# A macaron feed-forward layer: residual updates of four groups moved to ScalarE and accumulating DMAs, one more group in seven products

## The chip, the cores and the metric

The kernel runs on one core of a Trainium2 chip. The metric is device time in microseconds of one execution. The kernel before takes 1795.06 us, the median of three executions (1794.87 to 1795.85). About 0.2% of that, 3.6 us, is what a measurement can tell from no change.

A core has a matrix engine (TensorE, PE in the profile; its weight loads are listed as PEld), a vector engine (VectorE, DVE), an engine for pointwise functions (ScalarE, ACT), a general engine (GpSimd, POOL) and an engine that here only issues DMAs (SyncE, SP). Each runs its own instructions in order and waits for the others by semaphores. TensorE writes only to PSUM, which has eight banks of 128 x 512 float32; the DMAs cannot reach PSUM.

## The reference

One decoder layer on a sequence of 1024 tokens, width 1024, hidden width 2816, all in float32. Cut to what matters:

```
h = modulate(rms_norm(x, ffn1_norm), sh1, sc1)
x = x + 0.5 * g1 * ((silu(h @ w_gate) * (h @ w_up)) @ w_down)      # first feed-forward
h = modulate(rms_norm(x, mix_norm), sh2, sc2)
b, c, v, u = split(h @ w_in)                                       # mixer: a gated convolution and
x = x + g2 * (concat(norm(conv(b, c, v)), norm(ssm(u))) @ w_out)   # a diagonal state-space model
h = modulate(rms_norm(x, ffn2_norm), sh3, sc3)
x = x + 0.5 * g3 * ((silu(h @ w_gate2) * (h @ w_up2)) @ w_down2)   # second feed-forward
y = rms_norm(x, final_norm)
# sh, sc, g: nine vectors of length 1024 from silu(cond) @ w_mod + b_mod
```

## The kernel before, in words

Activations lie transposed: the residual x is 8 tiles of 128 channels (d) by two halves of 512 tokens (h), in SBUF throughout. A float32 product is made of three matmuls on rounded parts: every weight and activation is split into a high half (ScalarE casts it) and a low half (VectorE subtracts the high half), and `mm3` issues high x high, high x low and low x high. So weights cost ScalarE and VectorE one instruction each per tile of 128 x 1024, the class `Weights` does that and hands the tiles out in order.

The hidden width is worked off in 11 groups of 256. A plain group g of the first feed-forward is `gate_up` (names fa{g}g and fa{g}u, 64 calls of `mm3`) and `down_both`, which calls `down` (fa{g}d, 32 calls). `down` makes four outputs of 128 x 512 at a time in four PSUM banks of a ring of six (`ps`), and when they are done, VectorE adds each, times a gate, to x. In this kernel that is one instruction per output, 16 per group.

From group SEVEN_FROM on (6 in the first feed-forward, 1 in the second) gate and up use `seven`: a two-by-two block product from seven block products instead of eight. It needs sums of weights, which GpSimd makes in `combine`, and sums of activations (S1 to S4), which `combos` makes on VectorE, ScalarE and GpSimd while the last plain group runs. Its down-projection (`down2`) follows within the next group.

Beside the first feed-forward there is side work, nearly all on VectorE, written as generators: `side1` prepares constants of the state-space model (`ssm_base`), then eight batches of tables (`ssm_batch`), each with matmuls named kp and tp on TensorE that read the tiles cl and bl of VectorE, and small stores to DRAM; in between it reduces six of the nine modulation vectors from 1 MB weight blocks (`mod_block`, tiles wm). `Clock` sets where side work stands in the program: every call of `mm3` ticks it, and every `period` ticks one step of the first generator is issued. The period is 4 in the down-projection of group 0, then 3 in gate and up and 8 in down. Before the last plain group all that is left of the side work is issued at once, its memory (`es1`) is released, and the combinations start. The framework that builds the program then orders each engine's instructions itself, so neighbours in the code need not be neighbours on an engine. All DMAs of this kernel are issued from SP's queue.

Of the kernel before, what the change touches and what calls it, by code (L numbers as in the profile page):

```python
# [13 lines left out]
F32 = mybir.dt.float32  # L14
F32R = mybir.dt.float32r
I32 = mybir.dt.int32
AF = mybir.ActivationFunctionType
ALU = mybir.AluOpType
# [3 lines left out]
P = 128  # L22
D = 1024
S = 1024
HALF = 512
# [6 lines left out]
CH = 16  # L32
TAU = 8

SEVEN_FROM = (6, 1)
J = S // TAU
NB = 8
GB = G // NB
# [16 lines left out]
class Clock:  # L55
# [7 lines left out]
    def after(self, ticks, fn):  # L63
        self.n += 1
        bisect.insort(self.due, (self.now + ticks, self.n, fn))
# [151 lines left out]
def hymba_layer(ctx: ExitStack, tc, x_d, wm1_d, wmod_d, gu1_d, gs1_d, wd1_d, win_d, wout_d, glu_d, gu2_d, gs2_d, wd2_d, cols_d, cond_d, lam_d, bc_d, out_d):  # L217
    nc = tc.nc
    V, A, T, SP = (InOrder(tc, e) for e in (nc.vector, nc.scalar, nc.tensor, nc.sync))
# [16 lines left out]
    pools = {}  # L236
# [11 lines left out]
    def ps(name):  # L248
        return mm_ps.tile([P, HALF], F32, tag="mm", name=name)
# [14 lines left out]
    gate = const.tile([P, 3, KT], F32, name="gate")  # L264
# [3 lines left out]
    def plain(arrays):  # L268
        for a in arrays:
            granules.extend([[(len(srcs), 2 * q), (len(srcs), 2 * q + 1)] for q in range(2)])  # L270
            srcs.append(a)

    def stream(gu, gs, wd, m):

        plain(a for g in range(m) for a in (gu[2 * g], gu[2 * g + 1], wd[g]))
        for g in range(m, NGRP):
            j = len(srcs)
            inner = m < g < NGRP - 1
            srcs.extend([gs[g - m, 0], wd[g - 1], gs[g - m, 1]] if inner else [gs[g - m, 0], gs[g - m, 1]])
            seven = [(i, c) for i in (j, j + 1 + inner) for c in Weights.SEVEN]  # L280
            seven = [seven[i : i + 2] for i in range(0, 14, 2)]
            if inner:
                granules.extend(seven[:1] + [[(j + 1, 2 * q), (j + 1, 2 * q + 1)] for q in range(2)] + seven[1:])
            else:
                granules.extend(seven)
        j = len(srcs)
        srcs.extend([wd[NGRP - 2], wd[NGRP - 1]])
        granules.extend([(i, 2 * q), (i, 2 * q + 1)] for q in range(2) for i in (j, j + 1))

    stream(gu1_d, gs1_d, wd1_d, SEVEN_FROM[0])  # L290
    plain([win_d[i] for i in range(8)] + [glu_d] + [wout_d[i] for i in range(4)])
    stream(gu2_d, gs2_d, wd2_d, SEVEN_FROM[1])
    ws = Weights((V, A, SP, nc.gpsimd), srcs, granules, 2)
# [3 lines left out]
    x = [[xt[k // 2][h][:, k % 2, :] for h in range(2)] for k in range(KT)]  # L297
    clock = Clock(4)
# [6 lines left out]
    def mm3(out, w, k, act, first, last, tok=slice(0, HALF), more=False):  # L305

        hi, lo = wsel(w, k)
        ah, al = (a[:, tok] for a in act)
        T.matmul(out, lhsT=hi, rhs=ah, start=first, stop=False, skip_group_check=more)
        T.matmul(out, lhsT=hi, rhs=al, start=False, stop=False, skip_group_check=more)  # L310
        T.matmul(out, lhsT=lo, rhs=ah, start=False, stop=last, skip_group_check=more)
        clock.tick()
# [146 lines left out]
    def down(h, wd, groups, n, name, after):  # L459

        for d0 in range(0, KT, 4):
            outs = [ps(f"{name}d{d}_{h}") for d in range(d0, d0 + 4)]
            for q, a_tiles in enumerate(groups):
                for fi in range(2):
                    for i, o in enumerate(outs):
                        mm3(o[:], wd[2 * q + d0 // 4], 4 * fi + i, a_tiles[fi, h], q == fi == 0, q == len(groups) - 1 and fi == 1)
            for i, o in enumerate(outs):
                d = d0 + i
                V.scalar_tensor_tensor(out=x[d][h], in0=o[:], scalar=gate[:, n, d : d + 1], in1=x[d][h], op0=ALU.mult, op1=ALU.add)
                if after is not None:  # L470
                    after(d, h)

# [9 lines left out]
    def combos(act, name, homes):  # L482

        blocks.clear()
        while act[1] is None or len(act[1]) < KT:
            yield
        (a11, a12), (a21, a22) = [(act[h][:4], act[h][4:]) for h in range(2)]
        blocks.update(A11=a11, A12=a12, A22=a22, S1=[], S2=[], S3=[], S4=[])
        G_ = nc.gpsimd
        for k in range(4):  # L490
            f22, f21, f11 = whole(a22[k], f"f22_{k}", V), whole(a21[k], f"f21_{k}", V), whole(a11[k], f"f11_{k}", V)
            V.tensor_tensor(out=f22[:], in0=f21[:], in1=f22[:], op=ALU.add)
            blocks["S1"].append(split_act(f22[:], f"{name}S1_{k}", homes[0]))
            yield
            V.tensor_tensor(out=f21[:], in0=f11[:], in1=f21[:], op=ALU.subtract)
            V.tensor_tensor(out=f11[:], in0=f22[:], in1=f11[:], op=ALU.subtract)
            blocks["S2"].append(split_act(f11[:], f"{name}S2_{k}", homes[1]))
            yield
            blocks["S3"].append(split_act(f21[:], f"{name}S3_{k}", homes[2]))
            yield  # L500
        while "free" not in blocks:
            yield
        for k in range(4):
            f12, s2 = whole(a12[k], f"f12_{k}"), whole(blocks["S2"][k], f"s2_{k}")
            G_.tensor_tensor(out=f12[:], in0=f12[:], in1=s2[:], op=ALU.subtract)
            blocks["S4"].append(split_act(f12[:], f"{name}S4_{k}", homes[3]))
            yield
# [75 lines left out]
    def sums_opened():  # L583
        es = ExitStack()
        ws.sums_pool = es.enter_context(tc.tile_pool(name="sums", bufs=1))
        pools["first"] = es.enter_context(tc.tile_pool(name="first", bufs=1))
        ws.pump()
        return es
# [6 lines left out]
    es1 = ExitStack()  # L595
# [147 lines left out]
    ws.open(ring1, 1)  # L743
    raw2 = es1.enter_context(tc.tile_pool(name="raw2", bufs=1))
    sb = es1.enter_context(tc.tile_pool(name="sb", bufs=1))
    ssm = {}
    bps = []

# [262 lines left out]
    def gate_up(act, name, a_tiles):  # L1011

        for fi in range(2):
            (wg,) = ws.take()
            pg = [proj(wg, act[h], f"{name}g{fi}_{h}") for h in range(2)]
            ws.free()
            (wu,) = ws.take()
            for h in range(2):
                pu = proj(wu, act[h], f"{name}u{fi}_{h}")
                gu_evac(fi, h, pg[h], pu, a_tiles, f"{name}_{fi}_{h}")  # L1020
            ws.free()

    def down_both(a_tiles, name):
        wd = ws.take(2)
        for h in range(2):
            down(h, wd, [a_tiles], 0, name, None)
        ws.free(2)

    down_both(a_tiles, "fa0")
    first_seven = SEVEN_FROM[0]  # L1030
    for g in range(1, first_seven):
        a_tiles = {}
        if g == first_seven - 1:
            while clock.side:
                clock.step()
            clock.period = 4
            es1.close()
            movs["B"] = es1.enter_context(tc.tile_pool(name="movB1", bufs=12))
            clock.side.append(combos(act1, "h1", "BBBA"))
            ws.retire(ring1)  # L1040
        else:
            clock.period = 3
        gate_up(act1, f"fa{g}", a_tiles)
        if g < first_seven - 1:
            clock.period = 8
        else:
            blocks["free"] = True
            ring1_open.close()
            sums_open = sums_opened()
        down_both(a_tiles, f"fa{g}")  # L1050
# [9 lines left out]
    for h in range(2):  # L1060
        down(h, [w[0], w[2], w[1], w[3]], [a_last, a_prev], 0, "fa10", after1)
# [306 lines left out]
    for dh in range(2):  # L1368
        wd = ws.take(2)
        for h in range(2):  # L1370
            for tok in PIECES[h] if dh else WHOLE:
                for i in range(4):
                    d = 4 * dh + i
                    o = ps(f"fb10d{d}_{h}_{tok.start}")
# [23 lines left out]
def _arrays(i):  # L1398
# [5 lines left out]
    for n in (1, 2):  # L1404
        g, u = _tiles(i[f"ffn{n}_w_gate"][0]), _tiles(i[f"ffn{n}_w_up"][0])
        a[f"wd{n}"] = i[f"ffn{n}_w_down"][0].reshape(NGRP, 2, P, 2, 512).transpose(0, 2, 3, 1, 4).reshape(NGRP, P, 2, 1024)
        m = SEVEN_FROM[n - 1]
        a[f"gu{n}"] = np.stack([g, u], axis=2).reshape(NF, P, 2, 1024)[: 2 * m]
# [40 lines left out]
```

## Time and profile before

| | |
|---|---|
| median of three executions | 1795.06 us |
| profiled execution | 1797.88 us |
| its span | 1796.1 us |
| busy in the span | PE 1728.8, DVE 1209.6, ACT 490.4, POOL 248.4 us |
| stretch of the change | 84.8 us (start of fa0d) to 458.97 us (start of fa6g) |

The profile is one execution. Its page gives busy times by engine, the span in 40 slices, and the chain of work that ended last. Lists in order of time have the start and the time taken in microseconds, the engine, the source line, the operation, output and inputs by the program's names without their numbers, the shape and the count; in square brackets stands how long the engine was idle before, and what ended that. Almost every line number is 101, the helper through which the engines are called, so the names tell the places. Groups of instructions have the total busy time, the mean of one in nanoseconds, and the idle time ahead of them. A window's row has busy times of the engines in it, the granted TensorE clock (1.00 is full speed), and the share of the 16 DMA engines.

### The profile page before, as it was taken

What the parts mean: (1) busy time and instruction counts of PE and PEld (TensorE: products, weight loads), DVE (VectorE), ACT (ScalarE), POOL (GpSimd) and SP (SyncE); (2) the same over time, 40 slices, a digit from 0 to 9 for tenths busy, and PEclk for the clock granted to TensorE, in tenths of its full rate; (3) what the DMA queues carried; (4) which work ended last, traced back from release to release, by engine and by line L of the source; (5) the groups of instructions that cost most, each with busy time, mean ns of one, the idle gap of its engine ahead of it and who ended that gap; (6) DMA issues with size and microseconds to landing.
All of it is one profiled execution on the core that took longest, in us unless ns stands there. A gap on an engine that the chain in (4) does not pass through costs nothing.

```text
span 1796.1 us, 20089 instructions
## 1 busy us (share of the span) xinstructions
PE 1728.8 (96%) x7772; PEld 1424.8 (79%) x7772; DVE 1209.6 (67%) x2170; ACT 490.4 (27%) x750; POOL 248.4 (14%) x155
## 2 busy tenths in 40 slices
PE   4998999999999999999999999799999999999996
PEld 3787887887888888888888887588888888888885
DVE  7999999977566556644657548855665566556546
ACT  4311212222322323332114324232232223222331
POOL 0000000005212121200000110621112111211211
PEclk9999999999999999999999999899999999999997
DMA  7624666510111213125752101011111111111102
GB/s 310 232 63 149 209 215 217 182 69 24 47 47 48 71 47 107 52 74 169 228 150 67 47 24 41 30 47 49 67 49 48 50 68 48 47 51 68 48 24 94
DMA packets 58738, 165.03 MB, mean 92 GB/s; under 512 B 14353, under 2 KB 29969, under 8 KB 43922
## 3 DMA queue, kind: packets, MB, share of 16 engines
q1 hardware_dynamic: 58642, 163.74, 26.6%
q8 instruction: 61, 1.00, 0.2%
q14 instruction: 35, 0.29, 0.1%
HBM read 140.64 MB, written 18.87 MB: 89 GB/s over the span
## 4 chain that ended last, share of the span: by engine, by line
PE 83%; DVE 11%; POOL 2%; DMA 2%; ACT 1%; issue 1%; SPq 1%; DVEq 0%; ACTq 0%; POOLq 0%
PE wo L101 5%; PE b L101 2%; PE v L101 2%; PE u L101 2%; PE c L101 2%; PE fb10d L101 2%; PE fa10d L101 2%; DVE w L101 2%; PE fa2d L101 1%; PE fa4u L101 1%; PE fa2u L101 1%; PE fa5u L101 1%; PE fa0d L101 1%; PE fb8d L101 1%; PE fb7d L101 1%; PE fb6d L101 1%
## 5 line engine op out<-in xcount | busy, mean ns | idle before, releaser
L101 ACT CAST w<-raw 128x1024 fp32r<-128x1024 f32 (+1 forms) x203 | 171.6, 860 | 489.2 <-POOL raw L159 61.3
L101 DVE TENSOR_TENSOR w<-raw,w 128x1024 fp32r<-128x1024 f32 (+1 forms) x203 | 208.2, 1039 | 59.2 <-ACT w L101 56.7
L158 POOL TENSOR_TENSOR sums<-raw 128x1024 f32<-128x1024 f32 x30 | 83.4, 2779 | 1077.8 <-DVE w L101 627.0
L101 ACT CAST w<-sums 128x512 fp32r<-128x512 f32 x90 | 52.8, 619 | 144.3 <-PE fb0d L101 11.2
L101 DVE TENSOR_TENSOR w<-sums,w 128x512 fp32r<-128x512 f32 x90 | 59.7, 689 | 47.9 <-ACT w L101 47.5
L101 DVE CUSTOM_DVE_ANT_0 wm<-wm,cact 128x1024 f32<-128x1024 f32 x48 | 58.1, 1214 | 0.8 <-DMA wm<-in_wmod 0.8
L101 PE MATMUL wo<-oa,w 128*128 128x512 f32 x192 | 45.8, 392 | 0.6 <-DVE w L101 0.6
L101 PE MATMUL u<-h,w 128*128 128x512 f32 x192 | 44.9, 392 | 0.8 <-DVE w L101 0.8
L101 PE MATMUL v<-h,w 128*128 128x512 f32 x192 | 45.4, 393 | 0.0
L101 PE MATMUL c<-h,w 128*128 128x512 f32 x192 | 45.2, 392 | 0.0
L101 PE MATMUL b<-h,w 128*128 128x512 f32 x192 | 44.9, 392 | 0.0
L101 PE MATMUL wo<-ob,w 128*128 128x512 f32 x192 | 44.6, 390 | 0.0
L338 POOL TENSOR_TENSOR n3aq<-n3aq,n3aq 128x512 f32<-128x512 f32 x5 | 6.5, 1291 | 266.5 <-ACT n3aq L101 266.3
L101 PEld LDWEIGHTS u<-h,w 128*128 128x128 f32 x192 | 35.6, 188 | 9.1 <-DVE w L101 1.2
L101 PEld LDWEIGHTS wo<-oa,w 128*128 128x128 f32 x192 | 35.7, 188 | 8.6 <-DVE w L101 1.1
L101 PEld LDWEIGHTS wo<-ob,w 128*128 128x128 f32 x192 | 36.0, 188 | 7.5
L101 PEld LDWEIGHTS b<-h,w 128*128 128x128 f32 x192 | 35.7, 188 | 7.2
L101 PE MATMUL p<-h,w 128*128 128x512 f32 x144 | 36.2, 409 | 5.3 <-DVE h L101 2.9
L159 POOL TENSOR_TENSOR raw<-sums,raw 128x512 f32<-128x512 f32 x30 | 41.0, 1366 | 2.4
L101 PEld LDWEIGHTS c<-h,w 128*128 128x128 f32 x192 | 35.6, 188 | 7.1
L101 PEld LDWEIGHTS v<-h,w 128*128 128x128 f32 x192 | 35.5, 188 | 7.1
L160 POOL TENSOR_TENSOR sums<-raw 128x512 f32<-128x512 f32 x30 | 40.1, 1337 | 2.4
(1094 smaller groups left out, 4046.9 us busy)
## 6 DMA issues: line engine op xcount, KB each, us to landing
raw<-in_gs SPq DMA_DIRECT2D x30, 1024.0 KB, 4.8
wm<-in_wmod SPq DMA_DIRECT2D x24, 1024.0 KB, 5.3
raw<-in_wd SPq DMA_DIRECT2D x22, 1024.0 KB, 4.8
raw<-in_gu SPq DMA_DIRECT2D x14, 1024.0 KB, 5.0
mw<-in_wm SPq DMA_DIRECT2D x8, 1024.0 KB, 8.7
raw<-in_win SPq DMA_DIRECT2D x8, 1024.0 KB, 5.8
x<-in_x SPq DMA_DIRECT2D x8, 512.0 KB, 6.7
mw<-in_wmod SPq DMA_DIRECT2D x4, 1024.0 KB, 4.8
```

The costliest lines, as they stand in the source:

```text
L101: r = getattr(self.engine, name)(*args, **kw)
L158: self.G.tensor_tensor(out=f[:, :1024], in0=r[:, 512:1536], in1=r[:, :1024], op=ALU.subtract)
L159: self.G.tensor_tensor(out=r[:, 512:1024], in0=f[:, 512:1024], in1=r[:, :512], op=ALU.add)
L160: self.G.tensor_tensor(out=f[:, 1024:], in0=r[:, 1536:], in1=r[:, 512:1024], op=ALU.subtract)
L338: nc.gpsimd.tensor_tensor(out=a, in0=a, in1=sq[:, :n], op=ALU.add)
```

## The change

The updates of x in the plain groups no longer run on VectorE while a pool named upd is open, which is in groups 0 to 3. There ScalarE reads the output from PSUM, multiplies by the gate and writes it to one of three buffers in SBUF, and a DMA issued from GpSimd's queue adds that buffer to x in SBUF. In the last plain group, now group 4, VectorE updates x as before.

Seven products are used from group 5 on. So the side work has three groups instead of four between group 0 and the last plain group; its period becomes 2 in gate and up and 16 in down.

```
-SEVEN_FROM = (6, 1)
+SEVEN_FROM = (5, 1)
...
             for i, o in enumerate(outs):
                 d = d0 + i
-                V.scalar_tensor_tensor(out=x[d][h], in0=o[:], scalar=gate[:, n, d : d + 1], in1=x[d][h], op0=ALU.mult, op1=ALU.add)
+                g = gate[:, n, d : d + 1]
+                if "upd" in pools:
+                    t = pools["upd"].tile([P, HALF], F32, tag="upd", name=f"{name}up{d}_{h}")
+                    A.activation(t[:], o[:], AF.Copy, scale=g)
+                    nc.gpsimd.dma_start(out=x[d][h], in_=t[:], accum_op=ALU.add)
+                else:
+                    V.scalar_tensor_tensor(out=x[d][h], in0=o[:], scalar=g, in1=x[d][h], op0=ALU.mult, op1=ALU.add)
                 if after is not None:
                     after(d, h)
...
     sb = es1.enter_context(tc.tile_pool(name="sb", bufs=1))
+    pools["upd"] = es1.enter_context(tc.tile_pool(name="upd", bufs=3))
...
             es1.close()
+            del pools["upd"]
...
         else:
-            clock.period = 3
+            clock.period = 2
         gate_up(act1, f"fa{g}", a_tiles)
         if g < first_seven - 1:
-            clock.period = 8
+            clock.period = 16
```

## The prediction

> **What bounds the kernel now.** I read the page first (busy shares, the 40 slices, the chain), then the windows of the stretch that the change touches, then TensorE's and VectorE's lists in order of time, then the DMA issues.
>
> ```profile
> span 1796.1 us, 20089 instructions
> PE 1728.8 (96%) x7772; PEld 1424.8 (79%) x7772; DVE 1209.6 (67%) x2170; ACT 490.4 (27%) x750; POOL 248.4 (14%) x155
> DVE  7999999977566556644657548855665566556546
> POOL 0000000005212121200000110621112111211211
> PE 83%; DVE 11%; POOL 2%; DMA 2%; ACT 1%; issue 1%; SPq 1%; DVEq 0%; ACTq 0%; POOLq 0%
> ```
>
> TensorE is busy 96% of the span and carries 83% of the chain. VectorE is at nine tenths in slices 2 to 8 (45 to 360 us), where the side work runs, and GpSimd does nothing there. The next rows are the windows: start and end, length, then busy time of PE, PEld, DVE, ACT, POOL, granted clock, DMA share, GB/s. The first is the whole stretch from the first down-projection to the end of group 4, the next two are groups 2 and 3.
>
> ```profile
> 84.80:391.17 306.37, 299.09 (x1346) 244.25 (x1344) 292.74 (x747) 58.82 (x82) 0.00 (x0) 0.99 0.48 162
> 181.23:252.23 71.00, 70.42 (x325) 57.03 (x324) 68.86 (x122) 14.06 (x20) 0.00 (x0) 1.00 0.61 211
> 252.23:322.69 70.46, 68.60 (x314) 56.10 (x312) 66.89 (x121) 13.29 (x18) 0.00 (x0) 1.00 0.63 211
> ```
>
> VectorE works 292.7 of 306.4 us, TensorE 299.1: two engines almost level, TensorE ahead. ScalarE works only 58.8. So a microsecond of matmul removed is a microsecond gained, but only if VectorE keeps up. TensorE in order of time shows where it did not:
>
> ```profile
> 150.07 8.32 PE L101 MATMUL fa1d<-fa_0a,w 128*128 128x512 f32 x36
> 163.24 1.89 PE L101 MATMUL kp<-cl,bl 128*16 128x128 f32 x8 [4.84 <-DVE bl L101]
> 165.82 4.69 PE L101 MATMUL fa1d<-fa_0a,w 128*128 128x512 f32 x12
> 170.35 11.04 PE L101 MATMUL fa1d<-fa_1a,w 128*128 128x512 f32 x48
> 186.76 1.05 PE L101 MATMUL kp<-cl,bl 128*16 128x128 f32 x8
> 188.15 5.74 PE L101 MATMUL fa2g<-h,w 128*128 128x512 f32 x24
> 215.78 1.03 PE L101 MATMUL kp<-cl,bl 128*16 128x128 f32 x8 [0.58 <-DVE bl L101]
> 271.14 1.03 PE L101 MATMUL kp<-cl,bl 128*16 128x128 f32 x8 [0.38 <-DVE bl L101]
> 296.71 1.03 PE L101 MATMUL kp<-cl,bl 128*16 128x128 f32 x8 [1.48 <-ACT fa_0a L101]
> 391.17 11.04 PE L101 MATMUL fa5g<-h,w 128*128 128x512 f32 x48
> 402.05 11.04 PE L101 MATMUL fa5u<-h,w 128*128 128x512 f32 x48
> 458.97 2.88 PE L101 MATMUL fa6gA<-h,w 128*128 128x512 f32 x12
> 461.69 2.88 PE L101 MATMUL fa6gB<-h1S,w 128*128 128x512 f32 x12
> 163.00:166.00 3.00, 2.76 (x13) 1.98 (x14) 1.76 (x6) 0.57 (x1) 0.00 (x0) 0.50 0.89 211
> 170.00:174.00 4.00, 4.00 (x20) 3.30 (x19) 4.00 (x7) 0.00 (x0) 0.00 (x0) 1.00 0.25 76
> ```
>
> The first batch of state-space tables (kp, the matmuls on bl and cl) waits 4.84 us for VectorE's bl. Right after that idle stretch the granted clock is 0.50, and only by 170 us 1.00 again. The 0.38 to 1.48 us waits leave no such mark.
>
> **The change, part by part.**
>
> Group 5 in seven products. From start to start, 48 matmuls take 10.88 us (391.17 to 402.05) and 12 take 2.72 (458.97 to 461.69), 0.227 each either way. A plain group has 192 gate and up matmuls, a seven-product group 14 times 12, which is 168. That saves 24, so 5.44 us, on the engine that carries the chain. What else such a group brings (sums on GpSimd, half-width casts) already runs beside TensorE in groups 6 to 10, for which the same rows repeat without waits. The combinations move with it from group 5 to group 4 and keep their price.
>
> Residual updates. VectorE loses 16 updates in each of groups 0 to 3. ScalarE gets 64 evacuations in their place, and GpSimd 64 accumulating DMAs of 256 KB on a queue that this kernel did not use.
>
> ```profile
> L101 DVE SCALAR_TENSOR_TENSOR x<-fa0d,gate,x 128x512 f32<-128x512 f32 x16 | 11.9, 744 | 0.1
> L101 DVE SCALAR_TENSOR_TENSOR x<-fa1d,gate,x 128x512 f32<-128x512 f32 x16 | 11.3, 733 | 0.0
> L101 DVE SCALAR_TENSOR_TENSOR x<-fa2d,gate,x 128x512 f32<-128x512 f32 x16 | 11.0, 751 | 0.0
> L101 DVE SCALAR_TENSOR_TENSOR x<-fa3d,gate,x 128x512 f32<-128x512 f32 x16 | 10.8, 730 | 0.0
> L101 DVE TENSOR_TENSOR w<-raw,w 128x1024 fp32r<-128x1024 f32 x27 | 32.8, 1217 | 1.5 <-ACT w L101 1.2
> L101 DVE TENSOR_TENSOR f<-h 128x512 f32<-128x512 f32 x6 | 4.0, 684 | 0.0
> L101 DVE TENSOR_TENSOR f<-f,f 128x512 f32<-128x512 f32 x4 | 2.7, 684 | 0.0
> L101 DVE TENSOR_TENSOR h1S<-f,h1S 128x512 fp32r<-128x512 f32 x3 | 2.1, 684 | 0.0
> 162.49 0.69 DVE L101 TENSOR_TENSOR bl<-bl,blt 128x512 f32<-128x512 f32 x1
> ```
>
> Side work in three groups. VectorE's work from 84.8 us to the end of group 3 becomes: 292.7, less the updates (11.9+11.3+11.0+10.8 = 45.0), less group 4's own (16 updates at 0.74, 6 weight halves at 1.22, 8 gating steps at 0.68: 24.6), less the combinations that ran there (4.0+2.7+2.1 = 8.8). That is 214.3. TensorE's work to the same point is 96 down matmuls, three groups of 288, and eight blocks of tables at 1.39 (186.76 to 188.15): 960 at 0.227 = 217.7, plus 11.1 = 228.8. VectorE has 14.5 us to spare, and it idled 306.4-292.7 = 13.6 in the old stretch. So the two stay level, and there will be short waits. The shorter period (one step per 2 matmul triples instead of 3 during gate and up) puts more side steps there, and VectorE then recovers during the down-projection, which has no updates left. I charge 4 us for these waits, the middle of 0 (its idle time all avoidable) and 8 (the same lateness as at the first table, once more).
>
> The first table. In the new order VectorE has 16 updates, one weight half and two gating steps fewer ahead of bl; less the overlap of neighbours of about 0.07 (a 1.22 row starts 1.14 before the next) they were 16 x 0.67 + 1.14 + 2 x 0.61 = 13.1. bl ends about 163.2-13.1 = 150.1. TensorE reaches it after 22 instead of 36 matmuls, at 155.1. Small dependent steps that stood between updates now follow each other directly; I allow 3 us, and 2 remain. The wait goes, and with it the half clock: 4.84, plus the block's 2.58 (163.24 to 165.82) against 1.39, plus 12 matmuls' 4.53 against 2.72. Together 7.84 us. The three smaller waits (0.58+0.38+1.48 = 2.44) I count as gone too, the 4 us above standing in for their successors.
>
> The round trip. This is what no row shows. ScalarE may fill a fourth buffer only when the DMA of the first has landed, and it waits in order, with the weight casts and gating steps queued behind it. Four outputs finish per 24 matmuls, 5.44 us, there are six PSUM banks, and the last output of a down-projection takes the tenth's bank, 15.0 us after the first output is ready. Up to there the evacuations have gone round the three buffers three times. With 0.65 for an evacuation (0.60 and its start) and L from its end to the landing, TensorE waits once 0.75 + 3(L + 0.65) exceeds 15.0: at L above 4.1 us. Beyond that each microsecond costs 3 per down-projection, 12 over four.
>
> ```profile
> raw<-in_gs SPq DMA_DIRECT2D x30, 1024.0 KB, 4.8
> co_d<-rot SPq DMA_DIRECT2D x8, 256.0 KB, 5.9
> si_d<-rot SPq DMA_DIRECT2D x8, 256.0 KB, 2.4
> L101 ACT ACTIVATE fa_0sg<-fa1g 128x512 f32<-128x512 f32 x2 | 1.2, 598 | 5.2 <-PE fa1g L101 5.2
> L159 POOL TENSOR_TENSOR raw<-sums,raw 128x512 f32<-128x512 f32 x30 | 41.0, 1366 | 2.4
> ```
>
> Of the 256 KB transfers the fast ones take 2.4 and those behind other traffic 5.9. These are the ends. An accumulation reads its destination too: 768 KB more cost 2.4 us between the first and third row, so 0.8 for 256 KB, making 3.2. GpSimd must start it; its nearest row is a whole tile at 1.37, and I add 1.1. L = 4.3, nearest to the fast row plus these two, since the new queue does not stand behind the loads, though it shares engines that are 61 to 63% busy. That costs 12 x 0.2 = 2.4 us. ScalarE's own 64 x 0.6 = 38 us fit into an engine that is busy 59 of 306; no VectorE work hides them if it stalls.
>
> The Trainium skill, "DMA: Bandwidth & Descriptors", section "Anatomy of one DMA — SWDGE (gpsimd) path", fits 2.0 us plus bytes over 436 GB/s for a DMA issued from GpSimd: an estimate of 2.6 for 256 KB, at which nothing would wait and the time be 1783.4. The trace has 2.4 on the other queue; none here shows an accumulating one.
>
> **Sum.** 5.44 + 7.84 + 2.44 - 4 - 2.4 = 9.3 us gained. The profiled execution took 1797.88 (span 1796.1) against a median of 1795.06 (1794.87 to 1795.85); the differences are taken from the median: 1785.8, rounded to 1786.
>
> **Rivals.**
>
> Only the products count. bl also hangs on a table load that is issued after VectorE's preparation and behind 55 small zero-fills on SP's queue. If that load comes late, the first wait stays, and about 5.4 less small waits remain: 1790. For it: the 2 us margin. Against: the preparation itself ends 13 us earlier.
>
> The round trip is long (slower). Place: ScalarE at the fourth evacuation, then TensorE at the last output of each of four down-projections. It decides at L = 5.1, where 12 x 1.0 + 3 of half clock eat the 15.7 saved less what VectorE's waits overlap. At the 5.9 of the third group of rows, 12 x 1.8 = 21.6 is lost; VectorE catches up meanwhile, so its 4 go: 15.7-21.6, 5.9 slower, 1801. Each stall would be 5.4 us, longer than the 4.84 after which the clock fell, so up to 3.0 more four times: 1813. For it: engines 61 to 63% busy with loads that now have three groups instead of four. Against: the fast row, and 22 us of matmuls in which the loads are not constant.
> By the Trainium skill's "TensorE: Matmul & The Clock Gate", section "Part 1: The HAM clock gate", about 3.4 us without work halve the clock; the rows above agree (0.50 after 4.84 idle, nothing after 1.48), and by it the 1813 holds rather than the 1801.
> The Trainium skill's "SBUF — State Buffer", section "SBUF: two separate sides", adds that GpSimd cannot write descriptors while VectorE holds their shared port; no run here shows that yet.
>
> VectorE becomes the bound. If it idles twice its 13.6 us (loads that come later, dependent steps), 13.6-4 = 9.6 more is lost: 1795, no change. For it: 94% load over 229 us. Against: its lateness so far came at one place.
>
> **How the numbers follow.** Forecast 1786: 0.35. Products only, 1790: 0.18. VectorE bound, 1795: 0.09. Long round trip, 1801 to 1813: 0.38, the largest of the others, because the disputed price is multiplied by 12 and its rows span 2.4 to 5.9. About 0.2% (3.6 us) is what a measurement can tell. So faster 0.53, same 0.09, slower 0.38. Low end: all waits gone, 1795.1-15.7 = 1779.4, taken as 1780. High end: 1812, just under the price with half clock; the likeliest case's own range is 1780 to 1790.
>
> **What would show it.** Right: fa5g in twelves (A, B, C) instead of 48s; kp without a wait near 155 us; down-projections of groups 0 to 3 at 21.8 us; accumulating DMAs landing in about 4 us. Wrong: rows fa1d to fa3d with waits on ScalarE and granted clock under 1, ScalarE's evacuations waiting for DMA, or VectorE without a gap and kp waiting for bl in groups 2 and 3.

## The result

The changed kernel takes 1839.31 us (median of four executions, 1835.38 to 1841.88), the kernel before in the same session 1795.45 (1794.87 to 1796.25). The ratio is 1.0241 with a 95% interval of 1.0226 to 1.0255: 43.9 us slower, where 9 us faster was forecast and 1812 was the top of the range.

The page of the changed kernel, span and busy times:

```profile
span 1838.0 us, 20299 instructions
PE 1737.0 (95%) x7748; PEld 1425.0 (78%) x7748; DVE 1177.4 (64%) x2125; ACT 537.0 (29%) x825; POOL 311.5 (17%) x225
```

Its windows from one group's start to the next (start and end, length, busy PE, PEld, DVE, ACT, POOL, granted clock, DMA share, GB/s): the first down-projection, groups 1, 2, 3, the last plain group 4, and 264 matmuls from the start of group 5 in seven products. The row behind them is the last plain group of the kernel before, group 5.

```profile
84.86:108.92 24.06, 22.86 (x98) 17.71 (x97) 21.48 (x117) 11.94 (x18) 9.75 (x12) 1.00 0.94 206
108.92:184.68 75.76, 69.14 (x301) 56.16 (x300) 59.49 (x261) 22.29 (x32) 13.97 (x16) 0.95 0.72 183
184.68:278.54 93.86, 81.22 (x338) 62.08 (x336) 73.44 (x139) 27.25 (x41) 15.67 (x18) 0.91 0.86 243
278.54:361.21 82.67, 74.24 (x326) 58.39 (x324) 67.31 (x128) 23.95 (x35) 13.24 (x16) 0.96 0.83 234
361.21:442.08 80.87, 70.83 (x289) 57.54 (x288) 49.58 (x69) 20.89 (x33) 25.69 (x19) 0.92 0.21 54
442.08:501.92 59.84, 59.84 (x265) 49.55 (x264) 35.06 (x49) 17.49 (x28) 13.43 (x8) 1.00 0.14 53
```

```profile
391.17:458.97 67.80, 66.20 (x290) 53.80 (x288) 47.95 (x58) 16.68 (x26) 25.29 (x15) 1.00 0.09 32
```

At 501.92 as much matmul work is left as at the start of group 6 in the kernel before (458.97): 24 matmuls of group 6 are done, and 24 of group 5's down-projection are still to come. That is 42.95 us later; from there to the end the difference changes by only 1.1 us (spans 1838.0 and 1796.1). So the whole loss lies in these rows, and not in the last one. The kernel before has 71.0 and 70.5 us for groups 2 and 3 and 67.80 for its last plain group. VectorE is no longer close to full (73 of 94 us in group 2), the DMA engines are: 0.94, 0.72, 0.86 and 0.83 in groups 0 to 3, against 0.33, 0.36, 0.61 and 0.63 before. TensorE in order of time, the rows that matter:

```profile
157.51 1.05 PE L101 MATMUL kp<-cl,bl 128*16 128x128 f32 x8
179.46 5.39 PE L101 MATMUL fa1d<-fa_1a,w 128*128 128x512 f32 x15 [4.70 <-ACT fa1up L101]
189.35 1.34 PE L101 MATMUL kp<-cl,bl 128*16 128x128 f32 x8 [3.15 <-DVE bl L101]
269.38 1.65 PE L101 MATMUL fa2d<-fa_1a,w 128*128 128x512 f32 x3 [2.36 <-ACT fa2up L101]
351.42 1.65 PE L101 MATMUL fa3d<-fa_1a,w 128*128 128x512 f32 x3 [3.59 <-ACT fa3up L101]
417.50 6.49 PE L101 MATMUL fa4d<-fa_0a,w 128*128 128x512 f32 x18 [5.81 <-DVE x L101]
429.57 12.67 PE L101 MATMUL fa4d<-fa_1a,w 128*128 128x512 f32 x42 [4.22 <-DVE x L101]
```

The first table (kp, 157.51) no longer waits. New are two long waits in group 4, which has no DMA updates at all, and waits of the down-projections for ScalarE's evacuations. These come to 18.6 us in groups 0 to 3 (total, times, longest):

```profile
PE fa2d L101 <- ACT fa2up L101: 6.7, 6, 2.4
PE fa1d L101 <- ACT fa1up L101: 6.6, 2, 4.7
PE fa3d L101 <- ACT fa3up L101: 4.1, 2, 3.6
PE fa0d L101 <- ACT fa0up L101: 1.2, 2, 0.7
```

Behind the evacuations stand the DMAs. One of ScalarE's groups, then the DMAs' medians from issue to landing (group 3 has 3.9):

```profile
L101 ACT ACTIVATE fa1up<-fa1d,gate 128x512 f32<-128x512 f32 x16 | 11.0, 689 | 22.8 <-DMA x<-fa1up 20.3 <-PE fa1d L101 2.3
x<-fa0up POOLq DMA_DIRECT2D x16, 256.0 KB, 3.9
x<-fa1up POOLq DMA_DIRECT2D x16, 256.0 KB, 6.2
x<-fa2up POOLq DMA_DIRECT2D x16, 256.0 KB, 4.9
```

### The profile page after: what moved, and what is told of

It reads as the page before. It is cut to its first block, busy times and chain, and to the rows that moved or that the text cites. A ratio compares the mean times of both kernels' runs of the same rounds, so it can differ in the third digit from the quotient of the medians.

```text
span 1838.0 us, 20299 instructions
## 1 busy us (share of the span) xinstructions
PE 1737.0 (95%) x7748; PEld 1425.0 (78%) x7748; DVE 1177.4 (64%) x2125; ACT 537.0 (29%) x825; POOL 311.5 (17%) x225
## 4 chain that ended last, share of the span: by engine, by line
PE 71%; issue 14%; DVE 7%; POOL 5%; DMA 2%; ACT 1%; SPq 1%; POOLq 0%; DVEq 0%; ACTq 0%
PE wo L101 4%; PE b L101 2%; PE v L101 2%; POOL x L473 2%; PE c L101 2%; PE fb10d L101 2%; PE fa10d L101 1%; PE u L101 1%; PE fb8d L101 1%; PE fb7d L101 1%; PE fb6d L101 1%; PE fb5d L101 1%; PE fb4d L101 1%; PE fb3d L101 1%; PE fb2d L101 1%
## 5 line engine op out<-in xcount | busy, mean ns | idle before, releaser
L158 POOL TENSOR_TENSOR sums<-raw 128x1024 f32<-128x1024 f32 x32 | 88.3, 2758 | 753.9 <-DVE w L101 677.9
L101 ACT CAST w<-sums 128x512 fp32r<-128x512 f32 x96 | 56.3, 619 | 154.2 <-PE fb0d L101 10.3
L101 DVE TENSOR_TENSOR w<-sums,w 128x512 fp32r<-128x512 f32 x96 | 63.6, 688 | 51.1 <-ACT w L101 50.7
```

The costliest lines, as they stand in the source:

```text
L101: r = getattr(self.engine, name)(*args, **kw)
L158: self.G.tensor_tensor(out=f[:, :1024], in0=r[:, 512:1536], in1=r[:, :1024], op=ALU.subtract)
```

## The experiments

Three theories: T1, the way of an update through three buffers, GpSimd and the DMA engines costs; T2, VectorE does, since its side work is squeezed into three groups; T3, the last plain group loses by itself, through its combinations. All medians below stand against a median of 1794.8 to 1796.1 for the kernel before on the same chip. Where the text subtracts one median from another, the two may come from different chips, so about 1.3 us of the difference can be theirs. Three runs leave work out and do not compute the layer: plain DMAs, light side work, and evacuations without DMAs.

| run | us | ratio to before |
|---|---|---|
| the DMAs alone | 1841.47 | 1.0261 (1.0244 to 1.0278) |
| the schedule alone | 1826.65 | 1.0173 (1.0157 to 1.0188) |
| addition on GpSimd | 1865.75 | 1.0390 (1.0373 to 1.0407) |
| plain DMAs | 1821.44 | 1.0141 (1.0125 to 1.0157) |
| S4 on VectorE | 1830.18 | 1.0185 (1.0165 to 1.0204) |
| nine buffers | 1817.93 | 1.0116 (1.0099 to 1.0133) |
| half the DMAs | 1814.40 | 1.0100 (1.0085 to 1.0115) |
| nine buffers and S4 | 1808.72 | 1.0065 (1.0048 to 1.0082) |
| the same, side work 3 and 2 | 1813.80 | 1.0104 (1.0086 to 1.0122) |
| the same, side work 3 and 3 | 1815.56 | 1.0119 (1.0103 to 1.0134) |
| the same, light side work | 1809.57 | 1.0083 (1.0068 to 1.0097) |
| the DMAs alone, nine buffers | 1808.01 | 1.0070 (1.0057 to 1.0083) |
| evacuations without DMAs | 1793.86 | 0.9993 (0.9983 to 1.0003) |
| DMAs in group 0 | 1793.79 | 0.9991 (0.9982 to 0.9999) |
| DMAs in group 0, S4 | 1791.02 | 0.9980 (0.9971 to 0.9989) |
| DMAs in group 0, seven from 5 | 1812.30 | 1.0093 (1.0079 to 1.0107) |

**The DMAs alone and the schedule alone.** From the changed kernel, the old schedule with the new updates:

```
-SEVEN_FROM = (5, 1)
+SEVEN_FROM = (6, 1)
...
-            clock.period = 2
+            clock.period = 3
...
-            clock.period = 16
+            clock.period = 8
```

> Only the residual updates of groups 0 to 4 go to ScalarE and accumulating DMAs (80 of them); group 5 stays plain and the side work keeps its four groups. Theory T1 (the way of an update through ScalarE, GpSimd and the DMA engines with three buffers is what costs; after the change the stretches of groups 0 to 3 were about 48 us over their matmul work): slower than before by 25 to 45 us, 1820 to 1840. Theory T2 (the cost is VectorE's, with the side work squeezed into three groups): VectorE loses 80 updates and keeps its four groups, so within 5 us of 1795. Theory T3 (the combinations of the last plain group end late, 13 to 15 us) adds nothing here: the last plain group stays near its 67.8 us.

And the new schedule with the updates on VectorE (the three edits the other way, in the kernel before):

> Group 5 in seven products and the side work in three groups, the updates on VectorE as before. T1: groups 0 to 3 lose most of their 48 us, 1795 to 1810 in all. T2: VectorE has 64 updates more than after the change, 1830 to 1860. T3: the last plain group takes about 80 us, not 67.8, although no accumulating DMA is left; if it takes 68 to 70 us, the late combinations were the DMAs' doing.

Each half alone is slower by more than 30 us, and they don't add: 46.5 (with 80 DMAs, since group 4 has them too) and 31.7 against 43.9 together. Groups 2 and 3 and the last plain group of the schedule alone, in windows:

```profile
192.10:269.10 77.00, 71.60 (x325) 56.86 (x326) 76.93 (x142) 14.32 (x20) 0.00 (x0) 1.00 0.62 208
269.10:350.20 81.10, 72.61 (x326) 57.94 (x325) 80.35 (x148) 14.50 (x20) 0.00 (x0) 0.98 0.57 195
350.20:429.60 79.40, 69.57 (x289) 56.64 (x288) 48.42 (x69) 19.27 (x30) 22.41 (x15) 0.94 0.08 27
```

VectorE is busy 76.93 of 77.00 us: with its updates and the denser side work it is the bound, as T2 says, but only there. My expectation for T1 (1795 to 1810) was wrong because it forgot that; T2's own range (1830 to 1860) began too high, and T1's for the DMAs alone (1820 to 1840) ended 1.5 us too low. The last row settles T3's first half: 79.40 us without any accumulating DMA. Group 5 of the DMAs alone took 69.6 us, so that loss belongs to the move of the combinations.

**The addition on GpSimd, and plain DMAs.** In the place of the accumulating DMA:

```
-                    nc.gpsimd.dma_start(out=x[d][h], in_=t[:], accum_op=ALU.add)
+                    nc.gpsimd.tensor_tensor(out=x[d][h], in0=x[d][h], in1=t[:], op=ALU.add)
```

> The changed kernel with the accumulating DMA replaced by an addition on GpSimd (x plus the same ScalarE tile): same ScalarE work, same three buffers, no DMA. T1 in its DMA form (descriptor writing and transfer make the round trip long): groups 0 to 3 give back 25 to 45 us, 1795 to 1815. T1 in its ScalarE form (the evacuations queue behind other ScalarE work): within 10 us of 1839. T2: within 10 us of 1839 too, since VectorE's work is unchanged.

```
-                    nc.gpsimd.dma_start(out=x[d][h], in_=t[:], accum_op=ALU.add)
+                    nc.gpsimd.dma_start(out=x[d][h], in_=t[:])
```

> The changed kernel with plain DMAs in place of the accumulating ones (the residual addition of groups 0 to 3 is left out: x is overwritten). If the accumulation itself makes the transfers long (about 1.5 us of all sixteen engines for 256 KB), landing falls from a median of 4.3 to about 3 us and the time to 1800 to 1815. If GpSimd's writing of descriptors and the queue with its loads make it, landing stays within half a us of 4.3 and the time within 8 us of 1839. T2 and T3: no change, 1839.

The addition is the slowest of all, by none of the theories. VectorE's and GpSimd's lists in order of time show why:

```profile
109.45 0.18 DVE L101 TENSOR_TENSOR w<-w,lam 128x32 f32<-128x32 f32 x1
110.96 1.22 DVE L101 TENSOR_TENSOR pw<-ro_r,rr 128x32 f32<-128x32 f32 x1
114.60 2.62 DVE L101 TENSOR_TENSOR pa<-pw 128x32 f32<-128x32 f32 x2
119.64 0.17 DVE L101 TENSOR_TENSOR pw<-pa,pa 128x32 f32<-128x32 f32 x1
```

```profile
109.60 10.06 POOL L473 TENSOR_TENSOR x<-x,fa0up 128x512 f32<-128x512 f32 x8 [9.82 <-ACT fa0up L101]
```

While GpSimd adds (109.60 to 119.66), each small VectorE instruction takes 1.2 to 1.3 us, as long as one GpSimd addition (10.06 us for eight), and 0.17 right after. The run therefore says nothing of buffers. The Trainium skill, "SBUF — State Buffer", section "SBUF: two separate sides", has VectorE and GpSimd take their shared port as an exclusive lock for a whole instruction; this trace agrees.

Plain DMAs gained 17.9 us. 1821.4 lies between the two expected ranges, 6 us above the first: the accumulation matters, but is not all. The queue's rows (packets, MB, share of the sixteen engines from 84 to 365 us), plain and then accumulating (the run with nine buffers):

```profile
q0 software_dynamic: 5120, 16.78, 15.6%
x<-fa0up POOLq DMA_DIRECT2D x16, 256.0 KB, 2.7
```

```profile
q0 software_dynamic: 9216, 16.78, 33.5%
x<-fa0up POOLq DMA_DIRECT2D x16, 256.0 KB, 4.2
```

Of 281 us, 15.6% over 64 transfers is 0.68 us of all sixteen engines each; 33.5% is 1.47, with 144 packets instead of 80. An output leaves TensorE every 1.36 us in a down-projection (5.44 for four), so during a down-projection the updates alone ask for more than the engines have.

**S4 on VectorE, nine buffers, and both.** The twelve additions of S4 change their engine:

```
-        G_ = nc.gpsimd
+        G_ = V if name == "h1" else nc.gpsimd
...
-            f12, s2 = whole(a12[k], f"f12_{k}"), whole(blocks["S2"][k], f"s2_{k}")
+            f12, s2 = whole(a12[k], f"f12_{k}", G_), whole(blocks["S2"][k], f"s2_{k}", G_)
```

> The changed kernel with the twelve additions of S4 for the first feed-forward (f12, s2 and their difference) on VectorE instead of GpSimd, so that they neither wait behind the sums of gu tile 15 on GpSimd nor take 1.3 us each. T3 (S4's chain ends late, and VectorE holds its x updates behind S4's low halves): the last plain group falls from 80.9 us to 68 to 71, the time to 1826 to 1830. If the lateness of the accumulating DMAs or of the loads makes that group long: 1837 to 1841.

Two of three updates take one of the six temporaries:

```
-                    t = pools["upd"].tile([P, HALF], F32, tag="upd", name=f"{name}up{d}_{h}")
+                    t = pools["upd"].tile([P, HALF], F32, tag="upd", name=f"{name}up{d}_{h}") if (d + 8 * h) % 3 == 0 else t2k(f"{name}up{d}_{h}")
```

> The changed kernel with nine buffers in rotation for the updates (three of their own, six of the temporaries that stand idle in a down-projection). T1a (three buffers are too few for a burst of sixteen: PE waits 18.6 us for evacuations in groups 0 to 3, and its half clock comes on top): these waits go, 1810 to 1817. T1b (the sixteen DMA engines, 1.4 us for each update against an output each 1.36 us, are the bound, and what is late then is loads and tables): 1825 to 1840, with the waits under other names. T2, T3: no change.

> Nine buffers and S4 on VectorE together. If T1a and T3 are right and independent: 1797 to 1805, about the time of the kernel before. If T1b: 1812 to 1828.

S4 first. In the changed kernel, GpSimd's list around the last plain group, then VectorE's:

```profile
404.98 2.40 POOL L158 TENSOR_TENSOR sums<-raw 128x1024 f32<-128x1024 f32 x1 [37.29 <-PE fa4u L101]
407.35 1.72 POOL L485 TENSOR_TENSOR f<-h 128x512 f32<-128x512 f32 x1
...
425.89 1.59 POOL L511 TENSOR_TENSOR f<-f,s 128x512 f32<-128x512 f32 x1
```

```profile
425.26 1.10 DVE L101 TENSOR_TENSOR h1S<-f,h1S 128x512 fp32r<-128x512 f32 x1 [1.77 <-ACT h1S L101]
428.17 0.69 DVE L101 TENSOR_TENSOR h1S<-f,h1S 128x512 fp32r<-128x512 f32 x1 [1.80 <-ACT h1S L101]
428.77 2.72 DVE L101 SCALAR_TENSOR_TENSOR x<-fa4d,gate,x 128x512 f32<-128x512 f32 x4
```

GpSimd idles 37 us until the last up product of group 4 gives up the memory for the weight sums; then sums and S4 go interleaved until 427.5. VectorE, in order, has S4's low halves ahead of the updates of x, so four finished outputs wait until 428.8 and TensorE has no PSUM bank. In the kernel before the same first row stands behind the first up product of group 5, some 21 us ahead of that group's down-projection; here it stands at its start.

```profile
413.18 2.46 POOL L158 TENSOR_TENSOR sums<-raw 128x1024 f32<-128x1024 f32 x1 [411.88 <-PE fa5u L101]
```

With S4 on VectorE group 4 takes 71.9 us instead of 80.9 and the kernel 9.1 us less, each a little above the expected range. T3 holds.

Nine buffers gain 21.4 us (1817.9, one above T1a's range), and TensorE's waits for evacuations are gone. ScalarE's group 1 in that run waits for a DMA 2.8 us, not 20.3:

```profile
L101 ACT ACTIVATE fa1up<-fa1d,gate 128x512 f32<-128x512 f32 x16 | 10.6, 691 | 10.1 <-PE fa1d L101 6.9 <-DMA x<-fa1up 2.8 <-ACT fa1up L101 0.4
```

The landings themselves didn't get shorter (medians 4.2, 6.8, 8.0 and 4.6 us): what mattered was how many may be on the way. Both edits together give 30.6 us, the sum of 21.4 and 9.1. But 13 us to the kernel before remain, between the two expectations.

**Half the DMAs.** Every second update on VectorE again, three buffers:

```
-                if "upd" in pools:
+                if "upd" in pools and i % 2 == 0:
```

> The changed kernel with every second update on VectorE again and 32 accumulating DMAs in place of 64. T1 (an update keeps all sixteen DMA engines 1.4 us, more than the 1.36 us between two outputs): the engines are half used by them, PE's waits for evacuations go, 1808 to 1820. T2 (VectorE binds): VectorE gets about 23 us of work back (32 by 0.73), so at 1839 or above.

24.9 us gained, as T1 says; T2 had it the other way.

**What the other 13 us are.** All five runs here have nine buffers, and all but the DMAs alone have S4 on VectorE too. Two spread the side work over gate, up and down (the second has 3 in the place of the 2):

```
-            clock.period = 2
+            clock.period = 3
...
-            clock.period = 16
+            clock.period = 2
```

> Nine buffers and S4 on VectorE, and the side work stepped every third product of gate and up and every second of the down-projection, in place of every second and every sixteenth (all its steps still fit ahead of group 4). T2a (VectorE has enough time in groups 1 to 3, but the dense steps in gate and up make the tables and the group's own activations late, while the down-projections, freed of the updates, stand empty): the waits for tables (10.3 us) and for fa_0af and fa_0a (5.0 us) and their half clock go in large part, 1790 to 1800 from 1808.7. T2b (VectorE has too much work in all): within 4 us of 1808.7.

> The same with every third product in both, by which three steps are left and run in one go ahead of group 4: T2a 1792 to 1803, one to three us over the other; T2b within 4 us of 1808.7.

They are slower than 1808.7 by 5 and 7 us: the waits for activations nearly went (1.1 and 0), those of tables grew from 10.3 to 20.0 and 25.2 us. Of these 7.7 and 13.5 are the last batch, which slipped into group 4. In the first of the two runs group 2 did get shorter (77.6 us for 86.8), but groups 3 and 4 got longer (82.3 for 78.9, 83.1 for 70.9). So the reordering moved the waits, and T2a's time fell. The next halves VectorE's modulation work:

```
-            mod_vector(r[:, i, :], s[:, i : i + 1])
+            V.tensor_tensor_reduce(out=r[:, i, :HALF], in0=r[:, i, :HALF], in1=cact[:, :HALF], scale=1.0, scalar=0.0, op0=ALU.mult, op1=ALU.add, accum_out=s[:, i : i + 1])
```

> Nine buffers and S4 on VectorE, with the modulation products of the side work over half of their columns (half of each dot product left out: 48 instructions of 1.21 us become about 0.6 us; transfers unchanged). VectorE as the cause of what is left in groups 2 and 3 (T2a or T2b): 1790 to 1799. The sixteen DMA engines, 0.88 to 0.97 busy in these groups, as its cause (late loads): 1804 to 1810.

By the medians nothing is gained, 1809.6, and no execution reached 1799, so T2b fell as well. The profiled execution, 1804.05, is the shortest of its four; in it groups 2 and 3 take 13 us less than with whole products and group 4 takes 7.5 more. VectorE's longest waits in groups 0 to 3 of it (total, times, longest):

```profile
DVE wm L101 <- DMA wm<-in_wmod: 11.6, 4, 4.9
DVE bb L101 <- DMA prm<-in_bc: 10.9, 3, 4.6
DVE rott L101 <- DMA mi_d<-mi: 6.5, 2, 3.5
```

The time taken from its work (48 times 1.21 less 0.68, 25 us) came back as waiting for loads and table stores: 39 us against 15 in the run with whole products. The DMAs alone with nine buffers agree: 1808.0, and VectorE waits 19.5 us for wm, where the kernel before has 0.8.

> The accumulating DMAs alone (group 5 plain, side work in four groups), with nine buffers. T1a (three buffers): the 21.8 us of waits for evacuations in the run with three buffers go and their half clock: 1808 to 1816 from 1841.5, and less than 1800 only if the waits for tables were due to them as well. T1b (the engines' time): 1830 or more.

The deciding run keeps everything and drops the accumulating DMAs:

```
-                    nc.gpsimd.dma_start(out=x[d][h], in_=t[:], accum_op=ALU.add)
```

> Nine buffers and S4 on VectorE, with ScalarE's evacuations kept and the accumulating DMAs left out (the residual of groups 0 to 3 is not added). If the DMAs' share of the sixteen engines makes the rest: 1786 to 1793, with VectorE's waits for transfers gone (15.0 us in groups 0 to 3 with the DMAs). If the three-group side work makes it: 1803 to 1810.

1793.9, 14.9 us less (13.8 when each is taken against the kernel before on its own chip), one us above the first expectation. VectorE's 15.0 us of waits for transfers shrink to 0.6. Groups 2 and 3 with the DMAs (nine buffers and S4) and without:

```profile
173.70:260.50 86.80, 76.77 (x338) 60.78 (x337) 72.32 (x136) 24.71 (x38) 13.08 (x15) 0.94 0.88 262
260.50:339.40 78.90, 72.57 (x326) 58.04 (x325) 66.84 (x125) 23.33 (x36) 14.04 (x17) 0.98 0.91 260
```

```profile
173.10:249.90 76.80, 74.05 (x337) 59.04 (x336) 69.83 (x133) 25.38 (x39) 0.00 (x0) 0.98 0.68 234
249.90:323.90 74.00, 71.00 (x326) 56.94 (x325) 66.90 (x125) 24.71 (x37) 0.00 (x0) 1.00 0.61 213
```

The sixteen engines fall from 0.88 and 0.91 to 0.68 and 0.61, the groups by 10.0 and 4.9 us. The loads and table stores land sooner (medians from issue to landing, with the DMAs and without):

```profile
raw<-in_wd SPq DMA_DIRECT2D x4, 1024.0 KB, 9.0
mo_d<-cl SPq DMA_DIRECT2D x8, 256.0 KB, 9.4
```

```profile
raw<-in_wd SPq DMA_DIRECT2D x4, 1024.0 KB, 5.1
mo_d<-cl SPq DMA_DIRECT2D x8, 256.0 KB, 2.9
```

So the rest was the DMAs' share of the engines, taken from loads and stores. Two other causes can be set aside. GpSimd's issuing did not make VectorE's instructions longer: VectorE is busy 279.1 us from group 0 to group 4 with the DMAs and 278.4 without. And with nine buffers ScalarE still waits for some of them (5.4 us), but TensorE no longer waits for an evacuation.

**DMAs only where the engines are free.** The kernel before, its group 0 alone by DMA, nine buffers; then the same with S4 on VectorE; then that with seven products from group 5.

```
-                if "upd" in pools:
+                if "upd" in pools and name == "fa0":
```

> The kernel before (group 5 plain, side work in four groups), with only group 0's sixteen updates by ScalarE and accumulating DMAs, nine buffers. Where the accumulating DMAs ran alone with nine buffers, group 1 took 66.9 us (74.6 before), and groups 2 to 5 13 to 18 us more than before. If these later losses are due to the DMAs of groups 1 to 4: about 7.7 us faster than before, 1787 to 1790. If the gain of group 1 is only put off (the tables shifted, the same waits later): within 3 us of 1796.

> The same with S4 of the first feed-forward on VectorE. T3's price was 9 us with seven products from group 5; here the last plain group waits only 1.6 us: 0 to 3 us faster than group0.

> Group 5 in seven products, side work in three groups, S4 on VectorE, and accumulating DMAs in group 0 only. If the DMAs' share of the engines was what was left: 1790 to 1797. If the three-group side work with the updates on VectorE binds (the schedule alone was 31.7 us slower, 9 of them S4's chain): 1806 to 1814.

The stretch from fa0d to group 6 shrinks from 374.2 us to 369.5 (first) and 367.4 (second). These are single executions: the profiled one of the kernel before took 2.8 us more than its median, that of the first 3.2 less than its own, that of the second 1.7 more, so the medians below decide. In the second, TensorE waits 3.0 us in the stretch; group 1 takes 71.2 us, not the 66.9 hoped for, and its main waits are for its own updates, which are on VectorE:

```profile
PE fa1d L101 <- DVE x L101: 2.2, 2, 1.9
PE kp L101 <- DVE bl L101: 0.6, 1, 0.6
PE fa5d L101 <- DVE x L101: 0.2, 1, 0.2
```

The first, 1793.79, is 1.0 us below the kernel before and meets the second of its expectations (within 3 us of 1796), but not for its reason: no table waits more than 0.6 us later, and group 1 itself gains only 3.5 us. The second is 3.8 us faster, 1791.02, as expected 0 to 3 us under the first, and the only complete version here that is faster than the kernel before by more than the 0.2% that can be told from no change, if barely. The third meets its second expectation: in groups 2 and 3 VectorE is busy 75.8 of 77.4 and 78.8 of 79.5 us, the bound of the three-group schedule when the updates stay on it.

## Why the prediction was wrong

*Group 5 in seven, 5.44 us: right.* 59.84 us for 264 matmuls, where a plain group has 288 at the same 0.227.

*The first table, 7.84 us: right.* No wait at 157.51, expected near 155. In the changed kernel the waits for evacuations in the same group hide the gain; with nine buffers and S4 on VectorE, group 1 takes 66.9 us against 74.7 before, 7.8 less.

*Three smaller waits gone, VectorE's new ones 4 us: too low.* Without any DMA (evacuations only) 5.4 us of waits for activations remain in groups 2 and 3, and groups 2 and 3 take 76.8 and 74.0 us; in the changed kernel the tables waited another 4.5 us. The count of VectorE's work was good (221.7 us to the end of group 3, 214.3 foreseen), and its volume alone did not decide: halved modulation gained nothing by the medians.

*The round trip, 2.4 us: the step that failed.* The median landing over all 64 is 4.3 us, the very L that was taken. But the formula was put on one L for all: group 1 has 6.2, and single DMAs take up to 11.7. With each group's own median it gives 8.7 us (6.3 in group 1, 2.4 in group 2), where TensorE waited 18.6. The burst of sixteen, 1.47 us of all engines each against one output per 1.36, is a matter of throughput, which a latency with a threshold doesn't show; how much of the price is this and how much the spread of single landings was not separated. The term measures 21.4 us (nine buffers). The rival of the long round trip named the place and, with 21.6, nearly this price; it had 0.38. That the two numbers agree is partly luck: it took an L of 5.9 in all four groups, where the medians are 3.9, 6.2, 4.9 and 3.9. Its highest total, 1813, is 26 us short.

*"Shares engines that are 61 to 63% busy": left without a price.* The prediction noted it and charged nothing; it measures 14.9 us by late loads and stores, even with nine buffers. The rows that L was built on are plain transfers; a plain copy from GpSimd's queue takes half the engines' time of an accumulation (0.68 against 1.47 us).

*"The combinations move with it from group 5 to group 4 and keep their price": the second step that failed.* It is another 9.1 us. The trace of before shows GpSimd's first sum released by the first up product; that it would be the last one in group 4 was not looked up. The memory that it waits for is a slot in a ring that the weight tiles of each group shift; that this is why the release moved is read from the code, not tried.

The sum: forecast 1786.0; 19.0 more for the round trip (21.4 less the 2.4 charged), 14.9 for the engines, 9.1 for S4, in the order in which they were taken away, make 1829.0. The other 10.3 us to 1839.3 are what stands between evacuations without DMAs (1793.9) and the same by the forecast's terms (1783.4, the forecast without its 2.4 for the round trip): the last plain group at 70.8 instead of 67.8, VectorE's waits above and their half clock. How these 10 divide was not measured. Half clock is part of all the prices. The prediction reasoned from a wait of 4.84 us; in the changed kernel the granted clock is 0.50 behind shorter ones too: behind those of 4.70 us (180 to 183 us) and 2.36 us (269.5 to 272.5, with two shorter waits ahead of it), and behind that of 3.15 us,

```profile
190.00:193.00 3.00, 3.00 (x12) 2.23 (x10) 2.89 (x8) 2.16 (x4) 1.65 (x2) 0.50 1.00 255
```

and over groups 0 to 3 TensorE is busy 247.5 us for matmuls that take 233.8 without the DMAs.

## What to carry to other kernels

Price a DMA that takes over an engine's work first by the share of the DMA engines that it takes in the stage where it runs (an accumulation here twice that of a plain copy), then by how many may be on the way in the longest burst; a latency alone, taken at its median, hides both. When work moves to another stage, look up what releases each of its instructions there: its length stays, its price need not. What was worth keeping here was small: DMAs in the one down-projection where the engines had stood at a third (0.33), and S4 off GpSimd, together 3.8 us.

## What the runs showed of the hardware

A 256 KB accumulation within SBUF takes 144 packets and 1.47 us of all sixteen engines, a plain copy 80 and 0.68. GpSimd spends a median of 0.87 us on issuing an accumulation and 0.54 on a plain copy. With VectorE busy 21.5 of 24.1 us beside it, the mean of sixteen is at most 0.94, with single ones up to 1.48; so no more than that was seen of the lock on descriptor writing that the prediction mentioned. The lock between VectorE and GpSimd's own additions was seen, at 1.2 us for an instruction of 0.17. For plain DMAs from GpSimd the estimate of 2.6 us from the Trainium skill's "DMA: Bandwidth & Descriptors", section "Anatomy of one DMA — SWDGE (gpsimd) path", fits the medians of groups 0 and 3 (2.7 and 2.5), but not those of groups 1 and 2 (5.1 and 3.9), and no accumulating group, whose medians begin at 3.9.
